# One more merge pair as a seven-product block multiplication, and new prices in the attention's list schedule

## The chip, the cores and the metric

The kernel runs on one core of one Trainium2 chip. The metric is the device time of one execution in microseconds (us), as the median of the runs. The engines are TensorE (PE in the profile; its weight loads are PEld), VectorE (DVE), ScalarE (ACT), GpSimd (POOL) and SyncE (SP), which issues most DMAs; POOL issues some too.

## The reference, cut to what matters

A transformer block over 1024 tokens of width 1024, in float32: a recurrent mixer (mLSTM, 4 heads) and a sparse attention (8 heads in 2 groups) side by side, merged by gates, then a gated feed-forward part.

```python
proj = u @ w_in + b_in                       # u = rms_norm(x); 5408 columns
mq, mk, mv, mo, mi, mf, nq, nkv, ngate, merge = split_columns(proj, IN_SIZES)
y_m = mlstm_mixer(mq, mk, mv, mo, mi, mf, ...)
y_n = nsa_mixer(nq, nkv, ngate, ...)
branch = einsum('btnw,nwd->btnd', stack([y_m, y_n]), w_branch)
gates = sigmoid(merge.reshape(B, T, 2, D_MODEL))       # merge: 2048 columns
h = h + sum(gates * branch, axis=2) @ w_out
...                                          # gated feed-forward, final rms_norm
```

The attention has three branches for each query: over 63 compressed blocks, over all earlier tokens (with 16 of 16 blocks selected, this is plain causal attention), and over a window of 512 tokens. Each has its own softmax and its own gate.

## The kernel before

Every matmul operand is split into a high and a low part (two float32r tiles), and a product is three matmuls: high by high, high by low, low by high (`mm3`, lines 354 to 356). ACT writes the high part, and DVE or POOL subtracts it for the low part.

**First stage** (up to about 425 us). It computes the columns of `w_in`, laid out with columns on the partitions, in tiles of 128 columns by 1024 tokens. Most column tiles are made in pairs (`PAIRS`): two column tiles, two halves of the inner dimension and the two token parities form a 2 by 2 by 2 block product, which is done with seven block products instead of eight (Strassen's scheme in Winograd's form). A block product `q` is four inner tiles, each three matmuls of 128x512, so a pair is 7 x 12 = 84 matmuls where the plain product has 96. A pair also needs sums of its weight blocks (`sums`), splits (`prep`) and sums of the products as they leave PSUM (`evict`), on DVE and ACT. Each pair's result lies in two neighbouring slots of 1024 elements (`DSLOT`), and from there a merge pair (`mg`) is stored to DRAM (`d_mg`), the first eight with the sigmoid applied. `COLS` holds the biases as columns, `DB` their differences.

The order on each engine comes from `Plan`: the steps are written with their operands and costs in nanoseconds, and a list planner issues them in the order that its clocks give, with eight PSUM banks. After the last pair but one it is told to load the first operands of the attention (`first_loads`). At its end the first weight tile of the next stage is split (`first_merge`).

**Attention** (about 425 to 743 us). There are 32 units: four pairs of heads by eight blocks of 128 queries. Each unit makes scores for the window and compressed branches (`w`) and for the full one (`s`), for two heads (PE into a PSUM tile S, two of them); adds the bias and takes the row's extreme on DVE (`low`, line 1554), exponentials on ACT (line 1558), reciprocal sums (lines 1570, 1571) and scaling on DVE or ACT (lines 1579, 1577); transposes blocks of probabilities on PE (tile T, line 1618), splits them (ACT line 1623, DVE line 1627) and multiplies by the values (tile obank, lines 1635 and 1638). Behind the last unit of a head pair the next pair's queries, keys and bias rows are loaded into the same places.

A second list scheduler (class `Op`, `ready`, the loop behind it) simulates PE, ACT and DVE with prices for every operation and a latency `LAT` between engines, and emits the instructions in the order that this gives. Where PE's next operation would start over 120 ns late, it places a group of filler:

```python
if e == "PE" and not dn["done"] and dense_at() is not None:
    dst = max(clock["PE"], dense_at())
    if cand is None or cand[2] > dst + 120.0:
        cand = ((dst, (999, 0)), None, dst)
```

A group is one inner tile of dense work (three matmuls, tile d, one PSUM bank). The filler is, in order (`c_dense`): the merge columns from `MG0` to 15 as plain products (a column tile is 2 token parities x 8 groups, evicted on ACT, line 1456), then the 16 products of the first branch (`branch0`, 4 groups each), which multiply the gates in place (tile MX, DVE line 1478). With the third product from the end of the merges the mixer's output is loaded over one half of the tokens (`values`, line 1464, POOL's queue); with the first branch product the gates' rows are loaded (`gate_rows`, line 1469, SP's queue). At least 13 branch products are issued before the next stage, behind the list if they are not in it; those left over (`rest`) are done at the start of the next stage.

**After that** come the second branch, the output projection and the feed-forward part, with `Plan` again.

Of the kernel before, what the change touches and what calls it, by code (L numbers as in the profile page):

```python
# [8 lines left out]
F32 = mybir.dt.float32  # L9
# [5 lines left out]
P = 128  # L15
T = 1024
# [18 lines left out]
EPS = 1.0e-6  # L35
MM = 216.0
NTH = 3
MG0 = 10
EXPLN = "natural_log_exp_and_others"


# [131 lines left out]
def body(ctx, tc, a, out):  # L173
# [11 lines left out]
    cst = con.tile([P, 2, P], F32, name="cst")  # L185
    ident = cst[:, 0, :]
    causal = cst[:, 1, :]
    eps = con.tile([P, 1], F32, name="eps")
    nc.vector.memset(eps, EPS)
    warm = con.tile([P, 1], F32, name="warm")  # L190

    att_stack = ctx.enter_context(ExitStack())
    att = att_stack.enter_context(tc.tile_pool(name="att", bufs=1, side="right"))
# [7 lines left out]
    KLC = att.tile([P, 2, 64], F32R, name="KLC")  # L201
    COLS = con.tile([P, N_ROW], F32, name="COLS")
    NQB = con.tile([P, 4], F32, name="NQB")
    DB = con.tile([P, 16], F32, name="DB")
    RELS = con.tile([P, 2, NH], F32R, name="RELS")[0:33]
    BF = att.tile([P, MH], F32, name="BF")
    GCOL = att.tile([P, 32], F32, name="GCOL")
# [183 lines left out]
    for q, (kh, r) in {1: (0, 0), 2: (1, 0), 3: (1, 1), 4: (0, 1)}.items():  # L391
# [43 lines left out]
    gq.dma_start(RELT[0:32, :], a["rel_bias"])  # L435

    PAIRS = [("qk", 0), ("kw", 0), ("qk", 1), ("cv", 0), ("qk", 2), ("mg", 0), ("qk", 3), ("nq", 0),
             ("mg", 2), ("nq", 2), ("o", 0), ("o", 2), ("mg", 4), ("mg", 6), ("mg", 8)]
    DSLOT = [11, 0, 11, 0, 11, 0, 11, 0, 0, 0, 4, 0, 4, 6, 0]
    HSLOT = {1: lambda r: slot(6 + r), 7: lambda r: slot(11 + r), 9: lambda r: (RND, RMV)[r]()[:, 0:1024],  # L440
             10: lambda r: slot(6 + r), 11: lambda r: slot(11 + r)}
    HKEY = {1: lambda r: keys_of(6 + r), 7: lambda r: keys_of(11 + r), 9: lambda r: [("ND", "MVH")[r]],
# [166 lines left out]
    def cols():  # L609
        pm = pl.buf()  # L610
        step1("PE", 200.0, lambda: nc.tensor.transpose(pm.ap[:, 0:N_ROW], rows, ident[0:N_ROW, 0:N_ROW]), [bbb], [pm], after=20000.0)

        def go():
            nc.vector.tensor_copy(COLS, pm.ap[:, 0:N_ROW])
            nc.vector.tensor_scalar(NQB, COLS[:, R_NQ:R_NQ + 4], -0.125, None, ALU.mult)
            for o_, s_, x_, y_ in ((0, COLS, slice(4, 8), slice(0, 4)), (4, COLS, slice(R_MO + 1, R_MO + 4, 2), slice(R_MO, R_MO + 3, 2)),
                                   (6, COLS, slice(R_KV + 1, R_KV + 2), slice(R_KV, R_KV + 1)),
                                   (7, COLS, slice(R_KV + 4, R_KV + 5), slice(R_KV + 2, R_KV + 3)),
                                   (8, NQB, slice(1, 4, 2), slice(0, 3, 2)),
                                   (10, COLS, slice(R_MG + 1, R_MG + 10, 2), slice(R_MG, R_MG + 9, 2))):  # L620
# [802 lines left out]
    with ExitStack() as sc:  # L1423
# [240 lines left out]
                self.eng, self.dur, self.deps, self.emit, self.prio = eng, dur, deps, emit, prio  # L1664
                self.end, self.extra, self.alt = None, extra, alt

        LAT = 180.0
        chain = {"S": [], "T": [], "V": []}
        queues = {"PE": [], "ACT": [], "DVE": []}
        clock = {"PE": 0.0, "ACT": 0.0, "DVE": 0.0}  # L1670
# [13 lines left out]
        def build_s(u):  # L1684
            p, i = units[u]
            ops = {}
            for k, r in (("w", 0), ("w", 1), ("s", 0), ("s", 1)):
                b = {"w": 2, "s": 1}[k]
                box = {}

                def emit(u=u, k=k, r=r, box=box):
                    box["low"], box["exp"] = s_job(u, k, r)


                if b == 1:
                    n, parts = P * (i + 1), [min(512, P * (i + 1) - c) for c in range(0, P * (i + 1), 512)]
                else:
                    n, parts = P * nwin(i), [P * (nwin(i) - 1)] * (nwin(i) > 1) + [KB]
                cost = 2 * sum(max(109.0, m / 2.4 + 13.0) for m in parts)
                deps = []  # L1700
                if len(s_free) >= 2:
                    deps.append(s_free[-2])
                if u >= 2:
                    deps.append(("T", u - 2, b))
                if u % 8 == 0 and k == "w" and r == 0:
                    deps.append(("pair", p))
                deps += chain["S"]
# [3 lines left out]
                tt = push(Op("DVE", nr * 180.0 + 1.044 * n, [so], lambda box=box: box["low"](), (u, 1)))  # L1711
                s_free.append(tt)
                ex = push(Op("ACT", nr * 290.0 + 0.833 * n, [tt], lambda box=box: box["exp"](), (u, 1)))
                ops[k, r] = ex
                if r == 1:
                    part = 0 if k == "w" else 1
                    de = [ops[k, 0], ex]
                    todo = scale(u, part)
                    rs = push(Op("DVE", 400.0, de, todo[0][0], (u, 2)))
                    bl = [2, 2, 0, 0] if part == 0 else [1, 1]  # L1720
                    scd = {}
                    for bb, (fn, _) in zip(bl, todo[1:]):
                        nn = (ncmp(i), P * (i + 1), P * nwin(i))[bb]
                        scd.setdefault(bb, []).append(push(Op("DVE", 70.0 + 0.522 * nn, [rs], fn, (u, 2),
                                                               alt=("ACT", 230.0 + 0.833 * nn))))
                    for bb, v in scd.items():
                        ops["sc", bb] = v
            return ops

        def build_t(u, ops):  # L1730
            p, i = units[u]
            gr = t_groups(u)
            first = True
            for gi, (part, grp) in enumerate(gr):
                box = {}
                m = len(grp)
                last = gi == len(gr) - 1

                def emit(u=u, gi=gi, grp=grp, last=last, box=box):
                    _, box["hi"], box["lo"], box["pv"] = t_job(u, gi, grp, last)  # L1740

                deps = [o for b, _ in grp for o in ops["sc", b]]
                deps += chain["T"]
                t = push(Op("PE", 214.0 * m, deps, emit, (u, 0), "T"))
                chain["T"] = [t]
                for b, _ in grp:
                    last_t[u, b] = t
                nfr = 256.0 * m
                d2 = [t] + ([pv_ops[-NTH]] if len(pv_ops) >= NTH else [])
                hi = push(Op("ACT", 60.0 + 0.833 * nfr, d2, lambda box=box: box["hi"](), (u, 0)))  # L1750
                lo = push(Op("DVE", 75.0 + 1.044 * nfr, [hi], lambda box=box: box["lo"](), (u, 0)))
                t.extra = ("T", lo)
                dp = [lo]
                if first and u >= 2:
                    dp.append(("OC", u - 2))
                first = False

                def emit_pv(box=box):
                    box["fin"] = box["pv"]()

                dp += chain["V"]
                pv = push(Op("PE", 428.0 * m / 2, dp, emit_pv, (u, 3)))
                chain["V"] = [pv]
                pv_ops.append(pv)
                if last:
                    oc_ops[u] = push(Op("ACT", 270.0, [pv], lambda box=box: box["fin"](), (u, 0)))

        for u in range(NU):
            build_t(u, build_s(u))
# [9 lines left out]
        def ready(op, eng):  # L1779
            t = 0.0  # L1780
            for d in op.deps:
                d = dep_op(d)
                if isinstance(d, tuple):
                    e = pair_at.get(d[1])
                else:
                    e = d.end
                    if e is not None and d.eng != eng:
                        e += LAT
                if e is None:
                    return None  # L1790
                t = max(t, e)
            if op.extra is not None and len(talloc) >= 2:
                e = talloc[-2].end
                if e is None:
                    return None
                t = max(t, e + LAT)
            return t

        dstate = {"gate": 0.0, "op": None}
# [4 lines left out]
        def dense_at():  # L1804
            if dstate["op"] is not None:
                o = dstate["op"]
                return None if o.end is None else max(o.end + LAT, split_end.get(dn["next"][1], 0.0) + LAT)
            return dstate["gate"]

        def place_dense(t):  # L1810
            ev, evict = next(cd)
            dn["mid"] = evict is None
            end = clock["PE"] = t + 3 * MM
            dstate["gate"], dstate["op"] = 0.0, None
            if ev is not None:
                clock["ACT"] = max(clock["ACT"], t) + 950.0
                split_end[ev] = clock["ACT"] + 2600.0
            if evict is not None:
                e = dn["next"][0]
                pe = Op("PE", 3 * MM, [], None, (-1, 0))  # L1820
                pe.end = end
                o = Op(e, 587.0 if e == "ACT" else 680.0, [pe], evict, (-1, 0))
                queues[e].insert(0, o)
                dstate["op"] = o
                dn["next"] = next(cd, None)
# [882 lines left out]
    bb = {}  # L2708
# [68 lines left out]
```

## Time and profile before

| | |
|---|---|
| median of 3 runs | 1515.35 us (1514.84 to 1516.04) |
| span of the profiled execution | 1513.3 us (its own time is not listed apart from the span) |
| mean granted PE clock | 0.999 |
| PE busy, whole span | 1495.8 us |
| attention, 425.3 to 742.6 us: PE / DVE / ACT busy | 314.48 / 266.35 / 251.92 us |

The span is from the first to the last instruction. Busy time is a union over an engine's instructions. A matmul's end is modelled and overlaps the next one, so its cost in a row of matmuls is the distance between starts, not its duration. A row such as "DVE TL L1627 <- ACT TH L1623" says that the DVE instruction of line 1627, which writes tile TL, waited for the ACT instruction of line 1623.

### The profile page before, as it was taken

The page shows a single profiled execution, that of the slowest core. Times are in us where ns is not written, and L with a number is a line of the kernel's source. Part 1 is how long each engine was busy: PE and PEld are TensorE (multiplying, and loading weights), DVE is VectorE, ACT ScalarE, POOL GpSimd, SP SyncE. Part 2 cuts the span into 40 slices and gives each one's busy share as a digit, 9 for nine tenths or more (in the row PEclk, how much of TensorE's full clock was granted, in tenths as well). Part 3 has the DMA queues.
Part 4 walks back from the last instruction along what each step waited for, and adds up shares of the span by engine and source line. Part 5 has one row for each costly group of instructions (what it writes and reads, how often), then busy time and mean ns, then how long its engine had stood idle before and what let it go on. Part 6 is the DMA issues. An engine that isn't in the chain of part 4 may idle for free.

```text
span 1513.3 us, 22320 instructions
## 1 busy us (share of the span) xinstructions
PE 1495.8 (99%) x7566; PEld 1262.8 (83%) x7566; DVE 1137.3 (75%) x2411; ACT 829.1 (55%) x1753; POOL 311.3 (21%) x389
## 2 busy tenths in 40 slices
PE   8999999999999999999999999999999999999997
PEld 6888888888889888898888788888888888888886
DVE  8979888867678896989787997555555555785795
ACT  6325666657569796878654674333333333454453
POOL 3000000000312243232101422322222221413310
PEclk9999999999999999999999999999999999999999
DMA  8324664496943378442477966877787776999731
GB/s 278 112 78 143 204 211 147 139 262 188 227 148 73 93 103 235 152 103 50 130 222 181 213 122 134 151 138 138 176 157 138 138 139 139 271 303 177 155 96 56
DMA packets 236133, 239.25 MB, mean 158 GB/s; under 512 B 13458, under 2 KB 179744, under 8 KB 236019
## 3 DMA queue, kind: packets, MB, share of 16 engines
q1 hardware_dynamic: 157296, 169.96, 35.4%
q0 software_dynamic: 78432, 67.48, 29.7%
q8 instruction: 59, 0.97, 0.3%
q14 instruction: 56, 0.45, 0.1%
q10 hardware_dynamic: 290, 0.40, 0.1%
HBM read 185.26 MB, written 60.39 MB: 162 GB/s over the span
## 4 chain that ended last, share of the span: by engine, by line
PE 90%; DVE 4%; issue 2%; DMA 2%; ACT 1%; POOL 0%; SPq 0%; DVEq 0%; POOLq 0%; ACTq 0%
PE PS L355 15%; PE PS L356 15%; PE PS L354 15%; PE bk L354 8%; PE bk L356 8%; PE bk L355 8%; PE T L1618 4%; PE d L354 2%; PE obank L1638 2%; PE obank L1635 2%; PE d L355 2%; PE d L356 2%; DVE UT_float L1966 1%; DMA UT_float<-in_x 1%; DVE quad_float32r L1966 1%
## 5 line engine op out<-in xcount | busy, mean ns | idle before, releaser
L1966 DVE TENSOR_TENSOR UT_float<-PS,UT_float 128x512 f32<-128x512 f32 x115 | 78.2, 689 | 73.7 <-PE PS L356 73.4
L1627 DVE TENSOR_TENSOR TL<-T,TH 128x512 fp32r<-128x512 f32 (+1 forms) x184 | 103.3, 581 | 20.8 <-ACT TH L1623 19.5
L1623 ACT ACTIVATE TH<-T 128x512 fp32r<-128x512 f32 (+1 forms) x184 | 90.6, 510 | 36.2 <-PE T L1618 33.9
L355 PE MATMUL PS<-quad_float32r,whi 128*128 128x512 f32 x272 | 105.9, 390 | 0.6 <-DVE quad_float32r L1966 0.6
L354 PE MATMUL bk<-UT,op 128*128 128x512 f32 x240 | 95.7, 399 | 0.3 <-ACT S L1196 0.3
L356 PE MATMUL bk<-UT,op 128*128 128x512 f32 x240 | 93.6, 390 | 0.0
L355 PE MATMUL bk<-UT,op 128*128 128x512 f32 x240 | 93.5, 390 | 0.0
L355 PE MATMUL PS<-quad_float32r,wlo 128*128 128x512 f32 x208 | 80.9, 389 | 0.0
L355 PE MATMUL PS<-quad_float32r,sl_float32r 128*128 128x512 f32 x200 | 77.8, 389 | 0.0
L354 PE MATMUL PS<-quad_float32r 128*128 128x512 f32 x192 | 75.1, 391 | 0.0
L355 PE MATMUL PS<-quad_float32r 128*128 128x512 f32 x192 | 74.7, 389 | 0.0
L356 PE MATMUL PS<-quad_float32r 128*128 128x512 f32 x192 | 74.7, 389 | 0.0
L354 PE MATMUL bk<-T,op 128*128 128x512 f32 x180 | 72.2, 401 | 0.0
L356 PE MATMUL bk<-T,op 128*128 128x512 f32 x180 | 70.2, 390 | 0.0
L355 PE MATMUL bk<-T,op 128*128 128x512 f32 x180 | 70.2, 390 | 0.0
L1969 ACT ACTIVATE UT_float<-PS 128x512 f32<-128x512 f32 x54 | 31.7, 599 | 69.2 <-PE PS L356 68.6
L355 PEld LDWEIGHTS PS<-quad_float32r,whi 128*128 128x128 f32 x272 | 51.1, 188 | 11.4 <-DVE quad_float32r L1966 1.0
L1650 POOL DMA_DIRECT2D d_yn<-os x32 | 32.5, 1022 | 130.7 <-ACT TH L1623 34.9
L728 ACT ACTIVATE op<-S 128x512 fp32r<-128x512 f32 x52 | 32.4, 628 | 48.3 <-PE bk L355 36.6
L354 PE MATMUL d<-UT,whi 128*128 128x512 f32 x136 | 56.4, 415 | 1.3 <-ACT mg L1456 0.8
L1979 POOL DMA_DIRECT2D sl_float<-in_w_up x28 | 36.5, 1305 | 98.4 <-DVE whi L1966 48.5
L356 PE MATMUL d<-UT,wlo 128*128 128x512 f32 x136 | 53.5, 393 | 0.0
(1464 smaller groups left out, 4874.2 us busy)
## 6 DMA issues: line engine op xcount, KB each, us to landing
rp<-in_w_in SPq DMA_DIRECT2D x27, 512.0 KB, 4.3
d_gu<-UT_float SPq DMA_DIRECT2D x35, 256.0 KB, 3.1
d_rep<-d_row SPq DMA_DIRECT2D x8, 960.0 KB, 6.2
sl_float<-in_w_up POOLq DMA_DIRECT2D x28, 256.0 KB, 4.8
sl_float<-in_w_gate SPq DMA_DIRECT2D x21, 256.0 KB, 3.7
sl_float<-in_w_up SPq DMA_DIRECT2D x21, 256.0 KB, 3.1
rp<-in_w_in SPq DMA_DIRECT2D x20, 256.0 KB, 3.3
d_mg<-S SPq DMA_DIRECT2D x10, 512.0 KB, 7.4
```

The costliest lines, as they stand in the source:

```text
L354: nc.tensor.matmul(ps, ah, bh, start=first, stop=False)
L355: nc.tensor.matmul(ps, ah, bl, start=False, stop=False)
L356: nc.tensor.matmul(ps, al, bh, start=False, stop=last)
L728: step1("ACT", 525.0, lambda: nc.scalar.activation(h, src(), AF.Copy), [r], [b])
L1618: nc.tensor.transpose(pt[:, z, P * r:P * r + P], e, ident)
L1623: nc.scalar.activation(hl[0][:, 0:m], pt[:, 0:m], AF.Copy)
L1627: nc.vector.tensor_tensor(hl[1][:, 0:m], pt[:, 0:m], cast32(hl[0])[:, 0:m], ALU.subtract)
L1635: nc.tensor.matmul(po, vv, th[:, z, :], start=(st[1] + z == 0), stop=False)
L1650: low_half.append(lambda: nc.gpsimd.dma_start(dst, half(1), accum_op=ALU.add))
L1966: return pl.step(alts, lambda e: ENG[e].tensor_tensor(out_(), x(), y(), alu), reads, writes, **kw)
L1969: return pl.step((("ACT", cost),), lambda e: nc.scalar.activation(out_(), x(), fn), reads, writes, **kw)
L1979: pl.step((("Pool", 1000.0),), lambda e: nc.gpsimd.dma_start(dst(), src(), accum_op=ALU.add), reads, writes, lat=lat, kb=kb, nd=1, after=a ...
```

## The change

Merge columns 10 and 11 are no longer filler beside the attention but a sixteenth pair of the first stage, as seven block products. The slots of the last merge pairs move: the third merge pair (`mg`, 4) goes to slot 0, the fourth to slot 4, the fifth to slot 6, and the new one to slot 0. `first_loads` stays behind the last pair but one, which is now the fifth merge pair. The filler of the attention begins with column 12, so it has 64 merge groups and not 96. The bias differences get more room in `DB`; `eps` and `warm` share a tile.

Apart from that, the prices of the attention's list schedule change: the latency between engines, DVE's score reductions, sums and scalings, the value products and filler groups on PE, and small ones on ACT.

```diff
-MG0 = 10
+MG0 = 12
...
-             ("mg", 2), ("nq", 2), ("o", 0), ("o", 2), ("mg", 4), ("mg", 6), ("mg", 8)]
-    DSLOT = [11, 0, 11, 0, 11, 0, 11, 0, 0, 0, 4, 0, 4, 6, 0]
+             ("mg", 2), ("nq", 2), ("o", 0), ("o", 2), ("mg", 4), ("mg", 6), ("mg", 8), ("mg", 10)]
+    DSLOT = [11, 0, 11, 0, 11, 0, 11, 0, 0, 0, 4, 0, 0, 4, 6, 0]
...
-        LAT = 180.0
+        LAT = {"PE": 210.0, "ACT": 150.0, "DVE": 150.0}
...
-                cost = 2 * sum(max(109.0, m / 2.4 + 13.0) for m in parts)
+                cost = 2 * sum(max(109.0, m / 2.4 + 14.0) for m in parts)
...
-                tt = push(Op("DVE", nr * 180.0 + 1.044 * n, [so], ...
+                tt = push(Op("DVE", nr * 85.0 + 1.044 * n, [so], ...
-                ex = push(Op("ACT", nr * 290.0 + 0.833 * n, [tt], ...
+                ex = push(Op("ACT", nr * 275.0 + 0.84 * n, [tt], ...
-                    rs = push(Op("DVE", 400.0, de, todo[0][0], (u, 2)))
+                    rs = push(Op("DVE", 250.0, de, todo[0][0], (u, 2)))
-                        scd...push(Op("DVE", 70.0 + 0.522 * nn, ... alt=("ACT", 230.0 + 0.833 * nn))))
+                        scd...push(Op("DVE", 130.0 + 0.525 * nn, ... alt=("ACT", 185.0 + 0.84 * nn))))
...
-                t = push(Op("PE", 214.0 * m, deps, emit, (u, 0), "T"))
+                t = push(Op("PE", 218.0 * m, deps, emit, (u, 0), "T"))
-                hi = push(Op("ACT", 60.0 + 0.833 * nfr, ...
-                lo = push(Op("DVE", 75.0 + 1.044 * nfr, ...
+                hi = push(Op("ACT", 67.0 + 0.834 * nfr, ...
+                lo = push(Op("DVE", 68.0 + 1.044 * nfr, ...
-                pv = push(Op("PE", 428.0 * m / 2, dp, emit_pv, (u, 3)))
+                pv = push(Op("PE", 480.0 * m / 2, dp, emit_pv, (u, 3)))
-                    oc_ops[u] = push(Op("ACT", 270.0, ...
+                    oc_ops[u] = push(Op("ACT", 281.0, ...
...
-            end = clock["PE"] = t + 3 * MM          # MM = 216
+            end = clock["PE"] = t + 3 * 229.0
-                split_end[ev] = clock["ACT"] + 2600.0
+                split_end[ev] = clock["ACT"] + 3000.0
-                o = Op(e, 587.0 if e == "ACT" else 680.0, [pe], evict, (-1, 0))
+                o = Op(e, 571.0 if e == "ACT" else 607.0, [pe], evict, (-1, 0))
```

In these prices `n`, `nn` and `nfr` are elements of a row, `m` is the number of blocks, and `nr` is 2 for the window score with its compressed part and 1 for the full score.

More of the change, by code (lines that the diff above doesn't have):

```diff
@@ L187, in body @@
     causal = cst[:, 1, :]
-    eps = con.tile([P, 1], F32, name="eps")
+    two_ = con.tile([P, 2], F32, name="eps")
+    eps, warm = two_[:, 0:1], two_[:, 1:2]
     nc.vector.memset(eps, EPS)
-    warm = con.tile([P, 1], F32, name="warm")
     att_stack = ctx.enter_context(ExitStack())
@@ L203, in body @@
     NQB = con.tile([P, 4], F32, name="NQB")
-    DB = con.tile([P, 16], F32, name="DB")
+    DB = con.tile([P, 18], F32, name="DB")
     RELS = con.tile([P, 2, NH], F32R, name="RELS")[0:33]
@@ L619, in go @@
                                    (8, NQB, slice(1, 4, 2), slice(0, 3, 2)),
-                                   (10, COLS, slice(R_MG + 1, R_MG + 10, 2), slice(R_MG, R_MG + 9, 2))):
+                                   (10, COLS, slice(R_MG + 1, R_MG + 16, 2), slice(R_MG, R_MG + 15, 2))):
                 w_ = s_[:, x_].shape[-1]
@@ L1710, in build_s @@
                 nr, n = (2, n + ncmp(i)) if b == 2 else (1, n)
-                tt = push(Op("DVE", nr * 180.0 + 1.044 * n, [so], lambda box=box: box["low"](), (u, 1)))
+                tt = push(Op("DVE", nr * 85.0 + 1.044 * n, [so], lambda box=box: box["low"](), (u, 1)))
                 s_free.append(tt)
-                ex = push(Op("ACT", nr * 290.0 + 0.833 * n, [tt], lambda box=box: box["exp"](), (u, 1)))
+                ex = push(Op("ACT", nr * 275.0 + 0.84 * n, [tt], lambda box=box: box["exp"](), (u, 1)))
                 ops[k, r] = ex
@@ L1723, in build_s @@
                         nn = (ncmp(i), P * (i + 1), P * nwin(i))[bb]
-                        scd.setdefault(bb, []).append(push(Op("DVE", 70.0 + 0.522 * nn, [rs], fn, (u, 2),
-                                                               alt=("ACT", 230.0 + 0.833 * nn))))
+                        scd.setdefault(bb, []).append(push(Op("DVE", 130.0 + 0.525 * nn, [rs], fn, (u, 2),
+                                                               alt=("ACT", 185.0 + 0.84 * nn))))
                     for bb, v in scd.items():
@@ L1749, in build_t @@
                 d2 = [t] + ([pv_ops[-NTH]] if len(pv_ops) >= NTH else [])
-                hi = push(Op("ACT", 60.0 + 0.833 * nfr, d2, lambda box=box: box["hi"](), (u, 0)))
-                lo = push(Op("DVE", 75.0 + 1.044 * nfr, [hi], lambda box=box: box["lo"](), (u, 0)))
+                hi = push(Op("ACT", 67.0 + 0.834 * nfr, d2, lambda box=box: box["hi"](), (u, 0)))
+                lo = push(Op("DVE", 68.0 + 1.044 * nfr, [hi], lambda box=box: box["lo"](), (u, 0)))
                 t.extra = ("T", lo)
@@ L1765, in build_t @@
                 if last:
-                    oc_ops[u] = push(Op("ACT", 270.0, [pv], lambda box=box: box["fin"](), (u, 0)))
+                    oc_ops[u] = push(Op("ACT", 281.0, [pv], lambda box=box: box["fin"](), (u, 0)))
         for u in range(NU):
@@ L1787, in ready @@
                     if e is not None and d.eng != eng:
-                        e += LAT
+                        e += LAT[d.eng]
                 if e is None:
@@ L1795, in ready @@
                     return None
-                t = max(t, e + LAT)
+                t = max(t, e + LAT["DVE"])
             return t
@@ L1806, in dense_at @@
                 o = dstate["op"]
-                return None if o.end is None else max(o.end + LAT, split_end.get(dn["next"][1], 0.0) + LAT)
+                return None if o.end is None else max(o.end, split_end.get(dn["next"][1], 0.0)) + LAT[o.eng]
             return dstate["gate"]
@@ L1816, in place_dense @@
                 clock["ACT"] = max(clock["ACT"], t) + 950.0
-                split_end[ev] = clock["ACT"] + 2600.0
+                split_end[ev] = clock["ACT"] + 3000.0
             if evict is not None:
                 e = dn["next"][0]
-                pe = Op("PE", 3 * MM, [], None, (-1, 0))
+                pe = Op("PE", 3 * 229.0, [], None, (-1, 0))
                 pe.end = end
-                o = Op(e, 587.0 if e == "ACT" else 680.0, [pe], evict, (-1, 0))
+                o = Op(e, 571.0 if e == "ACT" else 607.0, [pe], evict, (-1, 0))
                 queues[e].insert(0, o)
```

## The prediction

> **What bounds the kernel now.** I read the page first, then the stretches around the change, then who waited there. The page: TensorE (PE) is busy nearly all the time, at full granted clock, and the chain that ended last is PE for nine tenths.
>
> ```profile
> span 1513.3 us, 22320 instructions
> PE 1495.8 (99%) x7566; PEld 1262.8 (83%) x7566; DVE 1137.3 (75%) x2411; ACT 829.1 (55%) x1753; POOL 311.3 (21%) x389
> ...
> PEclk9999999999999999999999999999999999999999
> ...
> PE 90%; DVE 4%; issue 2%; DMA 2%; ACT 1%; POOL 0%; SPq 0%; DVEq 0%; POOLq 0%; ACTq 0%
> ```
>
> The profiled span is 1513.3 us; the runs' median, 1515.35, is 2.05 above it. I take those 2.05 us as what lies around the span, unchanged.
>
> Two stretches matter: the end of the first stage, and the attention (425.3 to 742.6). Columns: the stretch, its length, then busy us (and instructions) of PE, PEld, DVE, ACT, POOL; clock, DMA share, GB/s.
>
> ```profile
> 340.00:380.00 40.00, 40.00 (x193) 33.21 (x192) 29.96 (x50) 28.61 (x40) 2.08 (x4) 1.00 0.67 193
> 380.00:425.30 45.30, 45.30 (x202) 37.52 (x201) 28.61 (x42) 20.43 (x25) 13.11 (x21) 1.00 1.27 254
> 425.30:742.60 317.30, 314.48 (x2076) 281.29 (x2075) 266.35 (x852) 251.92 (x676) 86.74 (x159) 1.00 0.46 107
> 742.60:800.00 57.40, 57.40 (x255) 47.54 (x254) 49.43 (x77) 29.40 (x49) 3.55 (x3) 1.00 0.75 225
> ```
>
> PE has no gap at the end of the first stage and 317.30 - 314.48 = 2.8 us of gaps in the attention, where VectorE (DVE) has 51 us idle. So a PE instruction taken out is worth its issue interval, as long as PE still always finds work. In the attention that work is filler: groups of three dense matmuls (merge columns, then the first branch product) put wherever the list schedule saw PE wait. The same stretches for the filler alone (tile d; PE, PEld, DVE, ACT) count three matmuls a group:
>
> ```profile
> 425.30:489.90 64.60, 25.51 (x93) 16.01 (x93) 0.00 (x0) 2.04 (x3) 1.00 0.30 75
> 489.90:500.70 10.80, 4.10 (x15) 2.60 (x15) 0.00 (x0) 0.69 (x1) 1.00 0.86 250
> 500.70:563.30 62.60, 20.48 (x72) 12.21 (x72) 0.00 (x0) 2.03 (x3) 1.00 0.39 61
> 563.30:583.30 20.00, 11.82 (x45) 7.86 (x45) 0.00 (x0) 1.35 (x2) 1.00 1.24 232
> 583.30:648.40 65.10, 24.30 (x88) 14.88 (x87) 1.38 (x2) 2.03 (x3) 1.00 0.60 176
> 648.40:661.40 13.00, 6.50 (x24) 4.15 (x24) 1.31 (x2) 0.00 (x0) 1.00 0.89 243
> 661.40:727.50 66.10, 25.95 (x90) 15.16 (x90) 4.88 (x8) 0.00 (x0) 1.00 0.19 39
> 727.50:742.60 15.10, 7.97 (x30) 5.21 (x30) 1.43 (x3) 0.00 (x0) 1.00 0.21 50
> ```
>
> 457 matmuls: 152 groups (96 of merges, 56 of 14 branch products) and one matmul of what follows. The short stretches are the gaps between head pairs, the one at 563.3 the longest, with 15 groups in 20 us.
>
> **The change, part by part.** *First stage, added.* Seven products of 12 matmuls, 84 in all:
>
> ```profile
> 368.32 0.39 PE L354 MATMUL bk<-UT,op 128*128 128x512 f32 x1
> ...
> 369.00 0.39 PE L354 MATMUL bk<-UT,op 128*128 128x512 f32 x1
> ...
> 578.07 0.39 PE L354 MATMUL d<-UT,whi 128*128 128x512 f32 x1
> ...
> 578.76 0.40 PE L354 MATMUL d<-UT,whi 128*128 128x512 f32 x1
> ...
> 561.65 0.60 PE L1618 MATMUL T<-cst,E14w 128*128 128x128 f32 x4
> 562.00 0.48 PE L354 MATMUL d<-UT,whi 128*128 128x512 f32 x1
> ...
> 562.78 0.39 PE L1527 MATMUL S15s<-S,S 128*128 128x512 f32 x1
> ```
>
> These are the first of three matmuls (lines 354 to 356) and the first of the next three, for the seven-product stage, for the filler back to back, and for filler behind transposes. In the first the starts are (369.00 - 368.32) / 3 = 0.2267 us apart, so 84 cost +19.04 us. Beside it, 18 DVE operations of about 0.69 (four sums, seven low halves, seven evictions: 12.4 us) and eight on ACT of about 0.63 (5.1 us):
>
> ```profile
> L781 DVE TENSOR_TENSOR S<-bk,S 128x512 f32<-128x512 f32 x27 | 18.3, 688 | 5.1 <-PE bk L356 4.7
> L728 ACT ACTIVATE op<-S 128x512 fp32r<-128x512 f32 x16 | 9.9, 628 | 13.5 <-PE bk L355 12.4 <-issue 1.2
> ```
>
> Both fit under 19.04 us of PE; without that cover the 12.4 us would be the price. SP issues two more loads and two more stores there (512 KB each) and loses as many loads, and four 256 KB stores, beside the attention; SP is no releaser of PE in either stretch, so nothing is charged.
>
> *Slots.* The third merge pair now lands in slot 0, right behind the last output-gate pair, whose final store from there is issued at 382.6 and lands up to 5.9 us later, at 388.5:
>
> ```profile
> L1074 SPq DMA_DIRECT2D d_y<-S x4: 319/372/430, 357.2 to 382.6; - x4
> ...
> DMA to landing us min/median/max: 5.0/5.5/5.9
> ```
>
> The new pair's evictions into the second row wait for that. PE reaches them from about 371 on, at 2.72 us a product; eight banks last 21.8 us, to about 393. No stall; ends 0 and +2, taken 0.
>
> *Attention, removed.* 32 groups. Back to back a group takes 578.76 - 578.07 = 0.69 us; directly behind transposes 562.78 - 562.00 = 0.78. So -22.1 to -25.0; most groups follow others or dense work, I take 0.70: -22.4. ACT loses two weight splits and four evictions, POOL eight subtractions; neither ends PE waits of weight.
>
> *The list's prices.* The list has PE queues in a fixed order, so they decide where filler stands. By the constants in the diff the score reductions get cheaper on DVE by 64 x 190 + 64 x 95 ns = 18.2 us, the reciprocals by 9.6, low halves and evictions by 2.3; the 141 scalings dearer by 8.6. Summed over the list (107.5 + 92.9 + 25.6 + 36.5 + 9.5 us before), DVE falls from 272 to 251 us, while PE's own part rises: 296 transposed blocks at 214 + 214 ns become 218 + 240, with the scores 196 and 205 us, and a group goes from 0.648 to 0.687. The old list was 196 + 152 x 0.648 = 295 us long if PE was full in it, with DVE 92% of that; it put in more filler than the chip needed, which is why DVE really idles 51 us. At 92% the new one is 273 us long, with room for (273 - 205) / 0.687 = 99 groups; at 87% it is 288, with 121. I take 110 of the 128 that are left. Fewer than 128 means that PE never runs dry; but the code puts at least 116 before the next stage, so six groups, 1.5 products, follow the list alone, each waiting for the one PSUM bank to be emptied. The nearest such wait is
>
> ```profile
> PE d L354 <- ACT mg L1456: 0.8, 1, 0.8
> ```
>
> so 1.5 x 0.8 = +1.2 us (ends 0 and, at 99 groups, four products, +3.4). Work left over runs in the next stage at the same interval, where PE has no gap: no difference.
>
> *Other PE gaps.* Now 2.8 us; ends -2.8 and +11 (first rival). Of an attention of some 288 us (317 less the 42 groups not placed, at 0.70) DVE needs the 266 above, so there is still slack: 0.
>
> Sum: +19.04 - 22.4 + 1.2 = **-2.2 us**, 1515.35 - 2.2 = **1513.1 us**.
>
> **Rivals.** (1) *VectorE sets the pace.* The new list prices a reciprocal step at 250 ns:
>
> ```profile
> L1570 DVE SCALAR_TENSOR_TENSOR rs<-sm,GT x64: 147/157/687, 430.8 to 731.4; 128x4 f32<-128x4 f32 x32, 128x2 f32<-128x2 f32 x32
> L1571 DVE RECIPROCAL rs<-rs x64: 167/174/182, 431.0 to 731.6; 128x4 f32<-128x4 f32 x32, 128x2 f32<-128x2 f32 x32
> ...
> L1579 DVE TENSOR_SCALAR E7w<-E7w,rs x2: 565/714/862, 492.3 to 493.1; 128x640 f32<-128x640 f32 x2
> ...
> L1579 DVE TENSOR_SCALAR E9w<-E9w,rs x2: 546/550/554, 512.2 to 512.7; 128x640 f32<-128x640 f32 x2
> ```
>
> 157 + 174 = 331 ns, so 64 x 81 = 5 us short, and the same scaling takes 550 or up to 862 ns; if one in ten of 141 is 0.3 longer, 4 to 6 us more. Up to 11 us late on DVE in a fixed order are PE gaps wherever the list is tight; half of it, +5: 1518.1 us. It speaks against it that DVE has 51 us idle now. The Trainium skill ("SBUF — State Buffer", section "SBUF: two separate sides") says that a VectorE operation in a two-port mode and a GpSimd operation lock each other out for the whole instruction; the spread of E7w against E9w agrees. By that rule alone, this rival's second part stays whatever the list says, which gives the same 1518.
>
> (2) *The filler runs out: slower.* If the list comes out no tighter than now, 128 groups are used up at the old rate: 112 by 661.4, the other 16 at 30 in 66.1 us, by 697. The last 46 us then have no filler; DVE was busy 9 tenths of such stretches, so they shrink by at most about 7, not by 24 x 0.70 = 17. +19.04 - 7 - 8 x 0.70 (two products no longer left over) = +6.4: 1521.8 us. It decides when the list has more than 205 + 128 x 0.687 = 293 us. The Trainium skill ("Perfetto Trace Analysis", section "Identifying the Most-Contended Engine") calls matmul busy a poor measure and weight-load busy a good one; by the rows above that is 89% in the attention, not 99%, so by that rule PE has a tenth of headroom there and filler taken out is not time taken out. PE's waits of 2.8 us speak for busy time here.
>
> (3) *Loads collide in the gap at 563.3: slower.* The two halves of the mixer output are loaded (POOL queue) with the 49th filler group, no longer the 81st, and the gate rows (SP) with the 65th. With 60 groups before that gap now, and some 45 to 55 then, the former fall into it, beside the next pair's keys and bias rows.
>
> ```profile
> L1464 POOL DMA_DIRECT2D UT<-d_y x4: 742/760/830, 589.2 to 591.5; - x4
> ...
> DMA to landing us min/median/max: 5.7/9.7/14.0
> ```
>
> They took 591.5 + 14.0 - 589.2 = 16 us alone. Issued ahead of the keys they would hold the pair back by up to 16 us; half, less what filler covers, is some +8: 1521 us. Behind the keys they cost nothing, the list having 16 merge groups first.
>
> (4) *The new order also closes PE's gaps*: +19.04 - 22.4 - 2.8 = -6.2, 1509.2 us.
>
> **Chances.** Forecast 0.60 (its own range 1509.5 to 1516.5, so 0.30 faster, 0.28 same, 0.02 slower), rival one 0.14 (0.09 same, 0.05 slower), two 0.08, three 0.08, four 0.07, a stall at slot 0 0.03 (0.02 same). Against 0.2%, 3 us, about what a measurement of this kernel tells from no change: faster 0.37, same 0.39, slower 0.24. Range 1509.0 to 1520.5.
>
> **What would show it.** First stage 19 us longer, PE without a gap near 371 to 393; attention 283 to 295 us, with DVE above 90% of it; 64 merge groups, none missing later; PE gaps in the attention of 2 to 6 us. I am wrong if PE gaps there pass 8 us, if PE stands at the start of the third head pair, or if the list's last stretch has no d rows.

## The result, and the profile after

The changed kernel takes 1531.87 us (median of four runs, 1531.14 to 1532.76) against 1515.22 before beside it: ratio 1.0108, 95% interval [1.0096, 1.0120]. It is 16.6 us slower, and 18.8 us above the forecast. The profiled execution took 1532.76 us, its span is 1531.0, so 17.7 us more of span are to be found. First the page of the changed kernel: the span, engines busy, the granted clock, the chain that ended last.

```profile
span 1531.0 us, 22312 instructions
PE 1500.2 (98%) x7554; PEld 1262.4 (82%) x7554; DVE 1147.4 (75%) x2433; ACT 827.0 (54%) x1751; POOL 303.9 (20%) x381
...
PEclk9999999999999998999999999999999999999999
...
PE 85%; DVE 7%; DMA 4%; issue 2%; ACT 1%; POOL 0%; SPq 0%; DVEq 0%; ACTq 0%; POOLq 0%
```

The clock has an 8 in the sixteenth slice (574 to 612 us), and DMA, 2% of the chain before, is 4%. Next the changed kernel by stage (stretch, length, busy us of PE, PEld, DVE, ACT, POOL; clock, DMA share, GB/s), and behind it the last stage of the kernel before:

```profile
380.00:445.05 65.05, 65.05 (x288) 53.86 (x288) 40.59 (x61) 25.39 (x34) 12.81 (x21) 1.00 1.01 212
445.05:759.10 314.05, 299.53 (x1980) 264.80 (x1979) 265.07 (x856) 245.85 (x667) 79.79 (x151) 0.98 0.43 102
759.10:1531.00 771.90, 761.46 (x3388) 629.93 (x3386) 522.61 (x867) 338.39 (x617) 193.29 (x174) 1.00 0.74 164
```

```profile
742.60:1513.30 770.70, 761.58 (x3388) 630.02 (x3386) 522.79 (x867) 338.52 (x617) 193.26 (x174) 1.00 0.74 164
```

The first stage is 445.05 - 425.30 = 19.75 us longer with PE full in it; the rest after the attention is 1.2 longer; the attention, which was to be 21 us shorter, is 317.30 - 314.05 = 3.25 shorter. It has 96 matmuls less, as it should, but PE's gaps are 314.05 - 299.53 = 14.5 us, not 2.8, and the clock in it is 0.98. The filler alone (tile d) in the gap ahead of the third head pair and in that pair:

```profile
575.80:595.50 19.70, 9.96 (x39) 6.89 (x39) 0.00 (x0) 0.69 (x1) 1.00 1.58 306
595.50:667.90 72.40, 18.05 (x61) 10.58 (x60) 2.74 (x4) 0.67 (x1) 0.93 0.50 139
```

The third pair takes 72.4 us where it took 65.1. The DMA share in the gap ahead, 1.58, was 1.24. Who waited for what, in the attention, on PE; and on ACT from 585 to 612 (total, times, longest us):

```profile
PE T L1618 <- DVE E16w L1579: 8.7, 1, 8.7
PE T L1618 <- DVE TL L1627: 3.1, 4, 1.8
```

```profile
ACT os L1644 <- DMA d_yn<-os: 12.4, 1, 12.4
```

One stall stands out. Its chain, back from PE, in the rows of the time line: PE's transposes wait for a scaling on DVE, that for the exponentials on ACT, and ACT had stood since 592 in front of one output copy.

```profile
579.34 2.25 POOL L1464 DMA_DIRECT2D UT<-d_y  x3
582.63 0.75 POOL L1464 DMA_DIRECT2D UT<-d_y  x1 [1.04 <-issue]
586.65 1.05 POOL L1650 DMA_DIRECT2D d_yn<-os  x1 [3.28 <-ACT TH L1623]
```

```profile
591.27 0.69 ACT L1456 ACTIVATE mg<-d,COLS 128x512 f32<-128x512 f32 x1 [1.26 <-PE d L356]
604.36 0.38 ACT L1644 ACTIVATE os<-obank 128x256 f32<-128x256 f32 x1 [12.40 <-DMA d_yn<-os]
```

```profile
607.99 0.47 PE L1618 MATMUL T<-cst,E16w 128*128 128x128 f32 x1 [8.65 <-DVE E16w L1579]
```

The 4 MB of values were issued at 579 to 583, behind the keys. The second store of unit 13 (the one that accumulates) follows them on POOL's queue at 586.65. The output copy of unit 15 needs that store's tile, of which there are two, and waits until it has landed. How long the stores of line 1650 took from issue to landing, issued from 583 to 600, and the values themselves:

```profile
L1650 POOL DMA_DIRECT2D d_yn<-os x2: 987/1020/1053, 586.7 to 596.2; - x2
...
DMA to landing us min/median/max: 8.4/13.0/17.6
```

```profile
L1464 POOL DMA_DIRECT2D UT<-d_y x4: 740/750/777, 579.3 to 582.6; - x4
...
DMA to landing us min/median/max: 15.7/19.3/21.4
```

17.6 us after 586.65 is 604.3, where ACT goes on. Behind the gap the clock is down (same columns as the stages):

```profile
600.00:605.00 5.00, 0.00 (x0) 0.00 (x0) 0.00 (x0) 0.65 (x2) 0.00 (x0) 0.80 0.73 195
605.00:610.00 5.00, 1.22 (x5) 0.93 (x6) 2.79 (x9) 3.42 (x16) 4.23 (x11) 0.50 0.05 13
610.00:615.00 5.00, 5.00 (x20) 4.00 (x20) 3.95 (x14) 3.86 (x13) 0.25 (x2) 0.68 0.43 87
```

The Trainium skill ("TensorE: Matmul & The Clock Gate", section "Part 1: The HAM clock gate") says that about 3.4 us without work bring the array to half clock, and as much work brings it back. The trace agrees: the last matmul before the gap ends at 599.3, and the granted clock is 0.50 from 603.0 to 613.3, until some 4 us after the work began again at 609.3.

### The profile page after: what moved, and what is told of

Same layout as the page of the kernel before. It is cut to its first block, busy times and chain, and to the rows that moved or that the text cites. A ratio compares the mean times of both kernels' runs of the same rounds, so it can differ in the third digit from the quotient of the medians.

```text
span 1531.0 us, 22312 instructions
## 1 busy us (share of the span) xinstructions
PE 1500.2 (98%) x7554; PEld 1262.4 (82%) x7554; DVE 1147.4 (75%) x2433; ACT 827.0 (54%) x1751; POOL 303.9 (20%) x381
## 4 chain that ended last, share of the span: by engine, by line
PE 85%; DVE 7%; DMA 4%; issue 2%; ACT 1%; POOL 0%; SPq 0%; DVEq 0%; ACTq 0%; POOLq 0%
PE PS L355 15%; PE PS L356 15%; PE PS L354 15%; PE bk L354 8%; PE bk L356 7%; PE bk L355 7%; PE T L1618 3%; PE obank L1638 2%; PE obank L1635 2%; PE d L354 1%; PE d L355 1%; PE d L356 1%; DMA d_yn<-os 1%; DVE TL L1627 1%; DMA d_h<-UT_float 1%
## 5 line engine op out<-in xcount | busy, mean ns | idle before, releaser
L354 PE MATMUL bk<-UT,op 128*128 128x512 f32 x256 | 101.9, 398 | 0.3 <-ACT S L1196 0.3
L356 PE MATMUL bk<-UT,op 128*128 128x512 f32 x256 | 99.8, 390 | 0.0
L355 PE MATMUL bk<-UT,op 128*128 128x512 f32 x256 | 99.8, 390 | 0.0
L354 PE MATMUL bk<-T,op 128*128 128x512 f32 x192 | 76.9, 400 | 0.0
L356 PE MATMUL bk<-T,op 128*128 128x512 f32 x192 | 74.9, 390 | 0.0
L355 PE MATMUL bk<-T,op 128*128 128x512 f32 x192 | 74.8, 390 | 0.0
L355 PEld LDWEIGHTS PS<-quad_float32r,whi 128*128 128x128 f32 x272 | 51.1, 188 | 11.5 <-DVE quad_float32r L1966 1.0
L781 DVE TENSOR_TENSOR S<-bk,S 128x512 f32<-128x512 f32 x72 | 48.4, 686 | 16.0 <-PE bk L356 15.0
L356 PEld LDWEIGHTS bk<-UT,op 128*128 128x128 f32 x256 | 48.1, 188 | 10.2
```

The lines of the kernel that those rows point to most:

```text
L354: nc.tensor.matmul(ps, ah, bh, start=first, stop=False)
L355: nc.tensor.matmul(ps, ah, bl, start=False, stop=False)
L356: nc.tensor.matmul(ps, al, bh, start=False, stop=last)
L781: step1("DVE", 605.0, lambda: nc.vector.tensor_tensor(y.at(), p3(), x.at(), ALU.add), [ps, x], [y])
```

## The experiments

Theory 1: the values, now beside the stores of the last units ahead of the third head pair, hold those stores back, and the stall is what the change loses. Theory 2: the pair's own loads do. Theory 3: the new list prices VectorE too low, and it falls behind.

### e1_os_elsewhere: the waiting copy gets another tile

```diff
-os_ = cp.tile([P, 256], F32, name=f"os{u}", tag="os", bufs=2)
+os_ = cp.tile([P, 512], F32, ..., tag="mg", bufs=1)[:, 0:256] if u == 15 else cp.tile(..., tag="os", bufs=2)
```

> The changed kernel, but the output copy of the last unit before the third head pair (unit 15) goes to the staging tile of the merge columns, not to the tile that unit 13's store still reads. Queue and bytes are as in the changed kernel. Theory 1 (the accumulating store of unit 13 lies behind the 4 MB of values on POOL's queue, lands at 604 us, and ACT waits 12.4 us for that tile): the store still lands some 17 us after its issue, but ACT's wait falls to under 4 us and PE's 8.7 us gap and the half clock behind it go: 1518 to 1521 us. Theory 2 (the third pair's keys and bias rows come late because 4 MB more share the transfers): nothing changes, 1530 to 1533. Theory 3 (VectorE falls behind a list that prices it too low): the wait only moves, 1528 to 1533.

1527.51 us, [1.0064, 1.0094] against before (here and below, the 95% interval of the ratio to the kernel before): 4.4 us back, not the 11 to 14 expected. PE's wait, and ACT's from 585 to 606:

```profile
PE T L1618 <- DVE E16w L1579: 4.7, 1, 4.7
```

```profile
ACT os L1644 <- DMA d_mg<-mg: 8.4, 1, 8.4
```

The link by unit 13's tile was real, but the copy now waits 8.4 us for the tile that it was given, whose store was issued on SP, not on POOL, and took those 8.4 us to land. In e5 below, without the values, a store that SP issued in this stretch (a smaller one, of output) landed in 2.0 us. So the values hold back stores of another queue too.

### e2_values_act and e8_values_sp: the same bytes on another queue

```diff
-nc.gpsimd.dma_start(UT[e][0][:, h::2], d_y[e][:, :, 512 * h:512 * h + 512])
+nc.scalar.dma_start(cast32(UT[e][0])[:, h::2], d_y[e][:, :, 512 * h:512 * h + 512])   # e2; nc.sync in e8
```

> The changed kernel with the four 1 MB loads of values issued by ACT instead of POOL (same place in the program, same bytes; they copy the words instead of rounding them on the way). Theory 1 (order in POOL's queue): the stores of units 13 and 14 land within about 8 us of their issue, no PE gap over 2 us at the start of the third pair, 1517 to 1521 us. Theory 2 (bandwidth): the loads still compete with the bias rows, the gap stays, 1528 to 1533. Theory 3 (VectorE priced too low): 1528 to 1533.

1531.95 us, [1.0094, 1.0124]: no gain, for another reason. ACT's queue and engine in the time line:

```profile
576.93 11.99 ACTq L1464 DMA_DIRECT2D UT<-d_y  x4
589.03 0.38 ACT L1623 ACTIVATE TH<-T 128x256 fp32r<-128x256 f32 x1 [11.52 <-issue]
```

ACT stood for 12 us while it issued four loads, and PE waited 10.5 us, until 589.9, for what ACT owed. One part of theory 1 did come: unit 13's store, issued at 587.5, lands in 6.8 us, not 17.6. But the time does not tell the theories apart; SP, which computes nothing, is the cleaner test.

> The changed kernel with the four loads at the same place issued by SP, which computes nothing (ACT stood for 12 us while it issued them). Bytes and time of issue stay, only the queue is another. By the order in POOL's queue alone the store of unit 13 lands in 3 to 6 us and the gap goes: 1518 to 1522 us. By the bytes alone (theory 1b's second part) the store still takes 7 us and more, and SP's own stores now lie behind the values: PE's gap 3 to 8 us, 1523 to 1531 us.

1531.04 us, [1.0089, 1.0119], at the upper end of the second forecast. PE's wait in the attention, the stores of line 1650 issued from 583 to 600, and POOL's time line:

```profile
PE T L1618 <- POOL E16c L1546: 9.7, 1, 9.7
```

```profile
L1650 POOL DMA_DIRECT2D d_yn<-os x1: 1007/1007/1007, 587.0 to 587.0; - x1
...
DMA to landing us min/median/max: 6.7/6.7/6.7
```

```profile
605.06 1.00 POOL L1650 DMA_DIRECT2D d_yn<-os  x1 [17.07 <-issue]
...
608.45 0.66 POOL L1546 MEMSET E16c<- 128x121 f32 x2
```

Off POOL's queue, unit 13's store lands in 6.7 us, not 17.6. But SP is now late with the first store of unit 14; the accumulating store must not overtake that one, POOL stands in front of it for 17 us, and the memset of unit 16 behind it in POOL's order holds the transposes. The stall keeps its size and changes its link. That fits what the Trainium skill states ("DMA: Bandwidth & Descriptors", section "Queues, rings and completion order"): each DMA engine goes round the queues that have work and takes each queue in order. By that, a store behind 4 MB in its own queue waits for all of it, one in another queue for its share; the 17.6 and 6.7 us agree.

### e5_values_out: the loads left out

```diff
-yield from merge(14, 1, {0: values})
+yield from merge(14, 1, {})
```

> The changed kernel without the four 1 MB loads of values: they are left out, so the first branch product reads old data; the order on all engines is as before it. Theory 1b (the 4 MB slow every store issued beside them, on POOL's queue most, on SP's by some 8 us; ACT waits for the tile of unit 13 and PE behind it): stores land within 3 to 6 us, no PE gap over 2 us at the start of the third pair, full granted clock there, 1517 to 1520 us, and the difference to the changed kernel, some 12 to 14 us, is what the loads cost by their place. Theory 2b (the third pair's own keys and bias rows are what holds the stores): the gap stays above 3 us, 1523 to 1531. Theory 3 (VectorE too low in the list): 1528 to 1533.

1519.38 us, [1.0019, 1.0040]: 12.5 us less than the changed kernel, as theory 1 in its wider form (1b) has it, and the stores of line 1650 land in 2.8 to 5.8 us. The stall is gone; PE's longest wait in the attention is 1.8 us. By stage:

```profile
444.75:747.00 302.25, 297.06 (x1979) 263.20 (x1979) 263.91 (x856) 246.04 (x667) 76.59 (x147) 1.00 0.41 91
747.00:1517.60 770.60, 761.43 (x3387) 629.69 (x3385) 522.35 (x867) 338.61 (x617) 193.27 (x174) 1.00 0.74 164
```

Against the changed kernel the attention is 314.05 - 302.25 = 11.8 us shorter. PE's gaps fall from 14.5 to 5.2 (9.3 us), and PE is busy 2.5 us less with one matmul fewer in the record; most of that is the half clock, at which PE worked from 609.3 to 613.3. After the attention another 1.3 us are gone.

### e6_values_later and e7_values_halves: the loads moved

```diff
-yield from merge(14, 1, {0: values})
-yield from merge(15, 1, {0: lambda: split(n + 2)})
+yield from merge(14, 1, {})                                        # e7: {0: lambda: values((0,))}
+yield from merge(15, 1, {0: lambda: (values(), split(n + 2))[1]})  # e7: values((1,))
```

> The changed kernel with the same four loads on the same queue, called eight filler groups later (first group of the last merge product instead of the one before it). Unit 13's store then goes ahead of them, and some eight groups are left as cover before the first branch product. Theory 1b: the store of unit 13 lands in 3 to 6 us, ACT has no wait above 3 us, 1517 to 1522 us, with 0 to 4 us of a new wait where the branch product needs the values. Theory 2b: the stall only moves, 1525 to 1532.

1523.08 us, [1.0034, 1.0068], with nothing left out: 8.8 us better than the changed kernel, and 1.1 above the range of theory 1b. Eight groups are enough to let unit 13's store go first; what is left of the stall is

```profile
PE T L1618 <- DVE E16w L1579: 1.7, 1, 1.7
```

and even this small gap, which ends at 600.2, has the clock down behind it: 0.72 from 600 to 605, and 0.50 from 602.2 to 605.6. That is a shorter gap than the 3.4 us without work cited above.

```profile
600.00:605.00 5.00, 4.36 (x18) 3.39 (x19) 4.46 (x17) 3.40 (x10) 2.08 (x8) 0.72 1.32 396
```

> The changed kernel with the first half of the values (2 MB) at its place and the other half eight filler groups later. Theory 1b: unit 13's store has 2 MB ahead of it and not 4, lands some 6 to 8 us after its issue and just about in time; PE's gap at the third pair 0 to 3 us, 1518 to 1523 us. Theory 2b: 1525 to 1532.

1527.54 us, [1.0065, 1.0095]: a miss, above the range of theory 1b. Half the bytes ahead of unit 13's store did not bring it through in time: issued at 586.2 it landed 12.4 us later. Those 2 MB run beside the pair's bias rows, which is the likely reason, though no run leaves the bias rows out. PE waited 3.7 us. So the pair's own loads probably have a part in it (theory 2), though in this order they stall nothing without the values (e5).

### e12_before_values_out: the same loads in the kernel before

The same edit as e5, in the kernel before.

> The kernel before without its loads of values (left out). They are issued there 6 us after the third pair has begun, with one wait of 2.9 us of ACT and no gap of PE. If they cost nothing there: 1514.5 to 1516 us, and the 12.5 us that they cost in the changed kernel come from their new place alone. If they cost something there too: 1510 to 1514.

1515.45 us, [0.9988, 1.0007]: they cost nothing there. The wait of ACT's output copies (line 1644) is in both traces, first before, then after (shortest, middle, longest ns):

```profile
L1644 ACTq EVENT_SEMAPHORE  x30: 38/38/2907, 456.9 to 738.4; - x30
```

```profile
L1644 ACTq EVENT_SEMAPHORE  x30: 38/38/13033, 476.3 to 754.8; - x30
```

Before, too, a store behind the values took 13.5 us to land; but they came 6 us after the third pair had begun, when the next copy that needed the tile was due late enough.

### e3_pair_alone and e4_prices_alone: the two halves of the change

> The sixth merge pair in the first stage alone, the list with its prices of before. At the old rate the 49th filler group, which carries the values, falls some four groups into the gap ahead of the third head pair, as it does in the changed kernel. Theory 1: the stores of the pair's last units wait behind the values again, a PE gap of 5 to 10 us there: 1526 to 1533 us. Theory 2: the same. Theory 3 (the new prices are what costs): 1513 to 1522, no gap, the filler used up before the list's end.

1539.53 us, [1.0142, 1.0176], 6.5 us above the highest forecast. The values did not fall into the gap as expected, but came before it, at 541.8. PE's waits in the attention, and the time after the last filler group:

```profile
PE d L354 <- DVE MX L1478: 11.1, 4, 9.4
```

```profile
725.90:766.40 40.50, 33.52 (x242) 29.48 (x240) 34.65 (x91) 33.60 (x82) 4.10 (x6) 1.00 0.13 21
```

Here it was the gate rows (MX) that fell into the gap, and the first branch product stood in PE's order until they came; and all 128 groups were used up by 725.9, so that 40.5 us ran without filler and PE idled 7.0 of them.

> The list's new prices alone, five merge pairs in the first stage as before. The values come with the 81st group, near the end of the third pair, away from the gap ahead of it. Theory 1: no stall at the start of the third pair; the values lie ahead of the fourth pair's queries on POOL's queue instead, a stall of 0 to 8 us there; about 34 groups are left to the end of the list and follow it one by one: 1516 to 1528 us. Theory 3 (the prices let VectorE fall behind): PE gaps in the attention of 8 us and more spread over the pairs, 1525 to 1533.

1533.22 us, [1.0099, 1.0129], just above the highest forecast. The list, and what follows it one by one:

```profile
425.30:725.50 300.20, 292.81 (x1954) 259.76 (x1953) 258.73 (x851) 241.44 (x660) 76.83 (x147) 0.99 0.47 109
725.50:759.40 33.90, 27.36 (x110) 20.07 (x111) 5.72 (x10) 6.30 (x11) 9.46 (x13) 1.00 0.74 252
```

The tighter list has no room for the filler of the old kernel: 36 groups follow it, with 6.5 us of PE idle. In the list PE's gaps are 7.4 us, and 4.0 of them are one wait for an output copy:

```profile
PE obank L1635 <- ACT os L1644: 4.0, 1, 4.0
```

ACT stood there until 645.2 for a store that POOL had issued at 631.5, right behind the values (624 to 631), and that took 13.6 us to land. This is the stall that theory 1 expects at the fourth pair; the 8 us of gaps spread over the pairs, which theory 3 expects, are not there. The pair alone costs 7.7 us more than the whole change; the prices alone cost about as much as the whole (1529.85 to 1535.04 against 1531.14 to 1532.76).

### e9, e10, e11: is it the price of a reciprocal step?

The list prices that step at 250 ns; in the trace its two operations take some 400 from start to start.

```diff
-rs = push(Op("DVE", 250.0, de, todo[0][0], (u, 2)))
+rs = push(Op("DVE", 400.0, de, todo[0][0], (u, 2)))    # e9: in e5; e10: in e6; e11: e10, and 545 for 480 in the value products
```

> The changed kernel without the loads of values (left out, as in the run before it that did so, 1519.4 us), and with one price of the list undone: a reciprocal step on VectorE at 400 ns, not 250. In the traces the pair of operations takes 194 + 215 = 409 ns from start to start. With 250 the list is 291.2 us long and places 118 groups; with 400 it is 299.0 us long and places all 128. Theory A (the underpriced step lets VectorE fall behind the fixed order, which is the 6 us by which the attention shrinks less than the groups taken out): PE's small waits fall by 3 to 6 us while the attention stays near 302 us with eight more groups in it: 1513 to 1516.5 us. Theory B (VectorE at 87% sets the pace whatever the list says, and filler fills what it leaves): the attention gets longer by the eight groups, 1518 to 1521 us.

1524.59 us, [1.0044, 1.0075]: above both ranges, and not faster than e5. The four executions spread from 1521.84 to 1526.97, with mean granted clocks from 0.998 down to 0.994; the profiled one is the fastest, so the trace explains only part of the median. By stage:

```profile
444.70:748.90 304.20, 299.13 (x2001) 266.89 (x1999) 263.29 (x845) 248.06 (x676) 76.00 (x147) 1.00 0.41 91
748.90:1520.10 771.20, 758.94 (x3365) 626.84 (x3364) 520.61 (x865) 340.98 (x620) 193.35 (x174) 1.00 0.75 164
```

PE's gaps in the attention, 5.1 us, are those of e5 (5.2): the 3 to 6 us of theory A did not come, and nothing here speaks for theory 3. Eight groups more cost 2 us there. The stage after has 22 matmuls less to do, 5.0 us, but is no shorter (771.2 against 770.6). In this execution PE waits twice, for 1.2 and 1.0 us, at 855.7 and 857.3, and behind that the clock is at half (same columns):

```profile
857.96:861.37 3.41, 3.41 (x9) 2.64 (x9) 2.60 (x6) 1.29 (x3) 1.60 (x2) 0.50 1.11 260
```

So what the eight groups save in that stage stays open.

> The changed kernel, complete, with values eight groups later and the reciprocal step at 400 ns. In the kernel with values later (1523.1 us) the loads still cost 3.7 us against none. Theory A: 1516 to 1520.5 us. Theory B: 1521 to 1526 us. If the new order puts the loads beside the stores again, 1526 and more.

1532.61 us, [1.0096, 1.0126]: the third case of that forecast. The order with 400 ns puts the values at 581 us again, into the gap, and

```profile
ACT os L1644 <- DMA d_yn<-os: 13.7, 1, 13.7
```

> As the run before, with the value products too at what the traces show, 545 ns and not 480 for two blocks (the two lines take 272 ns a block on average). The list is then 297.0 us long and places 110 groups, so some ten follow it one by one. Theory A: PE's waits in the attention fall further, the ten groups at the end add at most 2 us: 1515 to 1520. Theory B: less filler inside gives a shorter attention and the same sum: 1520 to 1525.

1530.48 us, [1.0084, 1.0117], above both ranges. PE's longest wait, until 591.5, is for an output copy, and this time it is not the values. They come at 595.7, as POOL's time line has it:

```profile
PE obank L1635 <- ACT os L1644: 6.9, 1, 6.9
```

```profile
577.14 1.03 POOL L1327 DMA_DIRECT2D S<-d_kl  x2
...
579.47 1.00 POOL L1650 DMA_DIRECT2D d_yn<-os  x1
...
595.74 3.03 POOL L1464 DMA_DIRECT2D UT<-d_y  x4
```

The store at 579.5, right behind the keys and beside the bias rows, landed 11.5 us later, and the copy two units on was due before. So theory 2 has its case too: without any values in flight the pair's own loads did it here, where the copy that needs the store's tile came soon enough. On the price both runs are inconclusive: whatever moves the list moves stores against loads, and that decides.

### e13_before_thinned: what is a filler group worth?

```diff
-mm3(ps, wh, wl, *rhs[k], k == 0, k == m - 1)
+if not (m == 8 and k in (2, 5) or m == 4 and k == 1 and done["n"] < 8):
+    mm3(ps, wh, wl, *rhs[k], k == 0, k == m - 1)
```

> The kernel before, its list and order untouched, with 32 filler groups left out at even distances (two of eight in each of 12 merge products, one of four in eight branch products; their sums are left out of the result, every eviction, load and store stays). The prediction took a group out of the attention at 0.70 us. Theory A (the new prices set an order that is too tight, and that costs the 6 us): in the old order, loose by 51 us of VectorE, 32 groups give 20 to 22.4 us: 1493 to 1496 us. Theory B (with fewer groups PE meets VectorE and ACT whatever the order, a group is worth some 0.47 us): about 15 us, 1498 to 1503 us.

1505.42 us, [0.9918, 0.9951]: 9.9 us for 32 groups (9.6 against the runs beside it), 0.31 us a group, less than either theory. By stage, and PE's waits:

```profile
425.30:731.70 306.40, 298.25 (x1979) 263.40 (x1978) 264.90 (x851) 250.32 (x675) 86.22 (x159) 1.00 0.48 113
731.70:1505.20 773.50, 763.28 (x3389) 631.58 (x3387) 523.16 (x867) 339.63 (x618) 193.30 (x174) 1.00 0.74 164
```

```profile
PE T L1619 <- DVE TL L1628: 2.3, 6, 0.8
...
PE d L354 <- ACT mg L1457: 1.3, 1, 1.3
```

The attention is 10.9 us shorter. The matmuls that are gone, 97 at 0.2267, are 22.0 us; 5.3 of them came back as gaps (8.15 against 2.8), and 5.8 as busy time of the matmuls that stayed (314.48 - 298.25 = 16.2, not 22.0), with no wait above 1.3 us. The matmuls did not get slower: back to back, three of them start 0.69 us apart before (578.07 to 578.76) and 0.68 here (730.35 to 731.03). Each is shown 0.39 us long, with a modelled end, so a wait of up to some 0.16 us behind one counts as busy. No stall hides in this: PE runs into ACT and DVE in many small places.

The stage after is 2.8 us longer here. In it PE waits 2.0 us for DVE, until 842.6 (in the kernel before its waits of this kind are two, 0.9 us together), and then the clock is at half:

```profile
843.47:846.88 3.41, 3.41 (x11) 2.84 (x11) 2.96 (x11) 1.88 (x5) 2.57 (x2) 0.50 1.12 234
```

That makes up the 2.8: some 1.1 us more of waiting, and half of 3.41. The profiled execution is the slowest of the four (1504.34 to 1506.95), so the 9.9 us of the median probably hold only part of it. In the attention alone a group is worth 10.9 / 32 = 0.34 us.

## Why the prediction was wrong

**The sum.** Forecast: +19.04 - 22.4 + 1.2 = -2.2. Measured, on medians: e13 gives 32 groups at -9.9; the pair's seven products add 19.75 in the trace; that is 1515.3 + 19.7 - 9.9 = 1525.1, and e5 is at 1519.4, so the order by the new prices is worth some -5.7 (by difference, with other groups left out than in e13; not run by itself); the values' place adds 12.5, to 1531.9. By the attentions of the two traces alone the order is worth less, 15.05 - 10.9 = 4.1, because the profiled execution of e13 lost time in the stage after.

**The step that failed first: "32 filler groups out of attention" at 0.70 each.** The prediction took PE's 2.8 us of gaps as proof that a PE instruction taken out is worth its issue interval. The 32 groups measured 9.9 us (10.9 in the attention alone), with the new order some 15 (317.30 - 302.25), not 22.4. In e5, as in e13, part came back as gaps (2.4) and part as longer busy time (22.0 less 17.4 is 4.6). The rule that the prediction weighed and set aside was the better guide: the Trainium skill ("Perfetto Trace Analysis", section "Identifying the Most-Contended Engine") takes weight-load busy for headroom, and that was 89% in the attention, a tenth of room. By it filler was not all time; the runs agree, and PE's few long waits were no evidence against it. It stood under rival two, with only the filler's end as its price.

**The step that failed worst: loads behind the keys "cost nothing".** Rival three had the place, the 49th group, and the loads; the 49th group did fall into the gap, and behind the keys, the order it held harmless. It asked only whether the loads delay the next pair. It did not ask who is queued behind them on POOL: the stores of the last units, and through their two tiles ACT. Its price, +8 from the forecast, was 12.5, and its chance, 0.08, was too small, since the prediction itself had the values fall into that gap (48 groups came before it).

**Point by point.** *First stage:* +19.04 forecast, 19.75 measured, PE full; from 371 to 393 it is busy 22.00 of 22.00 us, so slot 0 cost nothing, as said. *The list:* 110 of 128 groups within 99 to 121; the list placed 118 by its own simulation and two followed (120 stand in the trace), with no wait worth a row, so the +1.2 was 0. *Left-over work* at the same interval in the next stage: the change does not test it, since 14 branch products stand ahead of that stage as before (770.6 us in e5, 770.7 before). In e4 that stage has 12 matmuls more and is 2.6 us longer, about their interval (2.7); e9 leaves it open. *Other gaps:* 0 forecast, 11.7 measured, 2.4 without the values. *Rival one* (VectorE's prices): the reciprocal step is underpriced by more than said (400 ns against 250), but repricing it brought no fewer gaps in e9, the one run that tests it by itself. *Rival two* shows in e3, where the filler is used up by 725.9, and not in the change; the gate rows, which rival three also names, fall into the gap in e3. *Rival four* is out.

**What would show it.** Of the three marks for being wrong two came: gaps above 8 us (14.5), and PE standing at the start of the third head pair (8.65 us). The last stretch has its d rows. The attention was to take 283 to 295 us; it takes 314, and 302 without the values. DVE above 90% of it did not come: 265.07 of 314.05.

**No complete version is faster than the kernel before.** The best one is e6 at 1523.1. With 19.7 us in the first stage against at most 22.4 in the attention, the exchange had 2.7 us to win if every group had counted in full.

## What to carry to other kernels

Little waiting on the busiest engine does not price its instructions. Before you count work as time, take some of it out in the old order and measure: here the argument said 0.70 us a group and the chip gave 0.31 to 0.34. When a change shifts a hand-made order, list every DMA that rides on it with its new place, and for each ask what stands behind it in its queue, which tile that keeps, and which engine waits for the tile.

## What the runs showed of the hardware

Issuing four 1 MB loads held ACT for 12.0 us (e2) and SP for 11.75 (580.16 to 591.91 in e8, up to 6.2 us for one), where POOL issued them in 3 to 4 us; on ACT that time was lost to its computing. A PE gap of 1.7 us in e6 was followed by 3.41 us at half clock, and so was one of 2.0 us in e13; one of 1.8 us in e5, at 609, was not (1.00 in the windows around it).
